# Removal keys and keys transposed two chunks at a time in the RWKV-7 part of a one-core decoder trunk

## The chip, the cores and the metric

One NeuronCore of a Trainium2 chip runs the whole layer. The metric is the device time of one execution in microseconds (us). A change of less than about 0.2% cannot be told from none here.

## The reference

One layer of a hybrid decoder trunk on 1024 tokens of width 1024: `h += W_out [ HGRN2 | dilated window attention | RWKV-7 ]( W_in rmsnorm(h) )`, then a gated feed-forward with a causal convolution, then a gated per-token embedding, then a final RMSNorm. All in float32. The change is in RWKV-7 alone, four heads of 64:

```
def step(state, inp):
    r_t, w_t, k_t, v_t, kk_t, a_t = inp
    sa = jnp.einsum('bhvk,bhk->bhv', state, -kk_t)
    state = (state * w_t[:, :, None, :] + sa[..., None] * (kk_t * a_t)[:, :, None, :]
             + v_t[..., None] * k_t[:, :, None, :])
    return state, jnp.einsum('bhvk,bhk->bhv', state, r_t)
```

The kernel does not step through tokens. It takes 16 chunks of 64 tokens and builds, per chunk, small matrices from decayed versions of the removal keys (`-kk`, called `ar[..0..]`), of the receptances (`ar[..1..]`), of `kk*a` (called `bhat` or `be`), and of the keys (`khat` or `kh`), so that the state is carried from chunk to chunk by one matrix product each.

## The kernel before, in words

Features lie on partitions, tokens on the free axis. A pair of heads fills the 128 partitions (64 rows each), so the four heads are two passes, `p` = 0 and 1. Each pass has a preparation (`rwkv_prep`, `rwkv_inverse`: projections, decays, scores and the inverse of a triangular matrix, a long chain on VectorE with two trips through DRAM) and a main part (`rwkv_main`), which calls `rwkv_group` for four groups of four chunks.

A group first needs its operands with tokens on partitions. Before, `block_diag` (L609) copies each operand into a [128, 4, 2, 64] tile whose off-diagonal blocks are zero, head 0 in one half of the columns and head 1 in the other: `abd` from the removal keys by ScalarE (ACT), `bbd` from `bhat` and `kbd` from `khat` by GpSimd (POOL). TensorE then transposes each of the four chunks of each of the three tiles (L754) into a PSUM tile `pt`, and ACT copies each `pt` in one instruction (L755) into `xr` (its columns 0 to 127), `rb` (columns 128 to 255) and `kt`. The values `v` are already done in the other way: two transposes of 128 plain columns (two chunks) each (L758), and four ACT copies of quarters of 64 partitions x 2 chunks x 64 columns (L762), which put each head and chunk in its place in `vt`.

After these come, in this order on TensorE: `py` = AB x T (L785, copied to `Y` by ACT, L786), `sc` = the key scores (L790, which uses `kbd` as its weights), `pu` = the second half of the inverse (L795, waits for `Y`), `pk` (L800), `px` (L806), `pgm` (L813), `pn` (L818 and L819), and the chain over the four chunks (`pS`, `pyo`, L832 to L837), whose result ACT copies into `y` in quarters, as for `v` (L843). All PSUM tiles of this part come from one pool, `mx`, with four buffers; a new tile waits until ACT or VectorE (DVE) has read the one that held its buffer. POOL spreads the scores into `ABt` and half of `rb` (L770) and fills `addend` (L737 to L744).

The order of instructions on each engine is set by the framework's scheduler when the program is built. It fills TensorE's queue between the group's products with the dense projection products of later column blocks (L127, L129, L131, output `dp`), two halves of 512 columns at a time. The engines run their queues in order, so an early product that waits holds everything behind it.

Of the kernel before, what the change touches and what calls it, by code (L numbers as in the profile page):

```python
# [10 lines left out]
F32 = mybir.dt.float32  # L11
# [7 lines left out]
P = 128  # L19
# [60 lines left out]
class Trunk:  # L80
# [429 lines left out]
    def rwkv_prep(self, p, tp, lt, d, j):  # L510

        tc, nc, par = self.tc, self.nc, self.par
# [46 lines left out]
            nc.gpsimd.tensor_tensor(r2, r1, self.mhalf, ALU.pow)  # L559
            d["kr"] = r2  # L560

        ar = self.slots.tile([P, 16, 2, 64], F32, tag="rk_ar", name=self.nm("ar"), bufs=1)
        be, kh = self.slot("bhat"), self.slot("khat")
        d.update(ar=ar, be=be, kh=kh)

# [18 lines left out]
        mxp = self.mxp  # L584
# [4 lines left out]
        v = self.mix_in(4 + 3 * p, 4 + p, "v", hooks={2 * p: removal_keys})  # L589
# [130 lines left out]
    def rwkv_group(self, p, g, rp, d, y3, S):  # L720

        nc, mxp = self.nc, self.mxp
        cs = slice(4 * g, 4 * g + 4)
        ar, v, gC = d["ar"], d["v"], d["gC"]

        def c3(t):
            return t.rearrange("p (c i) -> p c i", i=64)[:, cs, :]

        def rt(name, shape, bufs=1):
            return rp.tile(shape, F32, tag=name, name=self.nm(name), bufs=bufs)  # L730

        ab = self.block_diag(rp, "abd", ar[:, cs, 0, :], nc.scalar)
        bb = self.block_diag(rp, "bbd", c3(d["be"]), nc.gpsimd)
        kb = self.block_diag(rp, "kbd", c3(d["kh"]), nc.gpsimd)
        if (rp, "add") not in self.bd:
            add = rt("addend", [P, 4, 2, 2, 64])
# [5 lines left out]
        for h in (0, 1):  # L742
            q = slice(64 * h, 64 * h + 64)
            nc.gpsimd.tensor_copy(add[q, :, 0, h, :], ar[q, cs, 1, :])  # L744
        abf, bbf, kbf = (t.rearrange("p c a b -> p c (a b)") for t in (ab, bb, kb))

        Xr = rt("xr", [P, 4, 192])
        RB = rt("rb", [P, 4, 256])
        Kt = rt("kt", [P, 4, P])
        Vt = rt("vt", [P, 4, 64])  # L750
        for src, dst in ((abf, Xr[:, :, 0:128]), (bbf, RB[:, :, 128:256]), (kbf, Kt)):
            pt = mxp.tile([P, 4, P], F32, tag="mx", name=self.nm("pt"))
            for u in range(4):
                nc.tensor.transpose(pt[:, u, :], src[:, u, :], self.ident)  # L754
            nc.scalar.copy(dst, pt)  # L755
        pt = mxp.tile([P, 2, P], F32, tag="mx", name=self.nm("pt"))
        for u in (0, 1):
            nc.tensor.transpose(pt[:, u, :], v[:, 256 * g + P * u:256 * g + P * u + P], self.ident)  # L758
        Vt4 = Vt.rearrange("p (b two) v -> p b two v", two=2)
        for h in (0, 1):  # L760
            for c in (0, 1):
                nc.scalar.copy(Vt4[64 * h:64 * h + 64, :, c, :], pt[64 * c:64 * c + 64, :, 64 * h:64 * h + 64])  # L762

        msk = self.msk.rearrange("p (m h i) -> p m h i", h=2, i=64)
        AB = rt("ABt", [P, 4, P])
# [3 lines left out]
        def spread(dst, src, m, eng):  # L769
            eng.tensor_tensor(dst.rearrange("p u (h i) -> p u h i", i=64),  # L770
                              src.unsqueeze(2).broadcast_to([P, 4, 2, 64]),
                              msk[:, m, :, :].unsqueeze(1).broadcast_to([P, 4, 2, 64]), ALU.mult)
# [13 lines left out]
        nc.scalar.copy(Y, py)  # L786
        spread(RB[:, :, 0:128], d["rb"][:, cs, :], 1, nc.gpsimd)
        ps = mxp.tile([P, 4, 2, 64], F32, tag="mx", name=self.nm("sc"))
# [21 lines left out]
        for hh in (0, 1):  # L810
            pg = mxp.tile([P, 2, 256], F32, tag="mx", name=self.nm("pgm"))
            for u in (0, 1):
                nc.tensor.matmul(pg[:, u, :], X[:, 2 * hh + u, 0:128], RB[:, 2 * hh + u, :], start=True, stop=True)  # L813
            nc.vector.tensor_tensor(GM[:, 2 * hh:2 * hh + 2, :], pg, addf[:, 2 * hh:2 * hh + 2, :], ALU.add)
        N = rt("N", [P, 4, 64])
        pn = mxp.tile([P, 4, 64], F32, tag="mx", name=self.nm("pn"))
        for u in range(4):
            nc.tensor.matmul(pn[:, u, :], RB[:, u, 128:256], X[:, u, 128:192], start=True, stop=False)  # L818
            nc.tensor.matmul(pn[:, u, :], Kt[:, u, :], Vt[:, u, :], start=False, stop=True)  # L819
# [3 lines left out]
        for u in range(4):  # L823
            c = 4 * g + u
# [4 lines left out]
            elif c < 15:  # L829
# [3 lines left out]
                nc.vector.scalar_tensor_tensor(Sn, pS, gC[:, c:c + 1], N[:, u, :], ALU.mult, ALU.add)  # L833
            nc.tensor.matmul(py[:, u, :], RB[:, u, 0:128], X[:, u, 128:192], start=True, stop=False)
            nc.tensor.matmul(py[:, u, :], RK[:, u, :], Vt[:, u, :], start=False, stop=S is None)
# [819 lines left out]
```

## Time and profile before

| what | us |
|---|---|
| median of 3 runs | 1521.87 (1519.84 to 1521.97) |
| the profiled execution | 1520.86 |
| its span in the profile | 1519.0 |
| main part of the first pass, by its transposes | about 147 to 217 |
| main part of the second pass | about 350 to 419 |

In the pages and rows PE is TensorE's products, PEld its weight loads, DVE VectorE, ACT ScalarE, POOL GpSimd, SP the queue that issues transfers. A row of the timeline gives start, length, engine, line, operation, output<-inputs, shape, and the count of instructions merged into the row; in brackets stand the idle time of the engine before it and what ended it. [...]

### The profile page before, as it was taken

To read this page: it belongs to the slowest core of one execution; us is meant where nothing else is said; L and a number is where in the kernel's file an instruction comes from. 1 tells how busy PE (TensorE), PEld (TensorE's weight loads), DVE (VectorE), ACT (ScalarE), POOL (GpSimd) and SP (SyncE) were. 2 spreads that over 40 slices of the span, in tenths; PEclk is the share of its full clock that TensorE was granted. 3 is DMA by queue.
4 is the path that set the end of the run, shared out by engine and by line. 5 is a ranking of instruction groups with operands and counts; after the bars stand their busy time and mean duration, and the time that the engine had idled before them with its cause. 6 is when DMAs were issued, how large, how long until landed. Compare 5 with 4: busy or idle time off the path is not lost. (4 is left out here: it accounts for less than half of the span.)

```text
span 1519.0 us, 20098 instructions
## 1 busy us (share of the span) xinstructions
PE 1468.0 (97%) x7452; PEld 1213.5 (80%) x7452; DVE 1087.5 (72%) x1574; ACT 634.8 (42%) x1091; POOL 431.6 (28%) x360
## 2 busy tenths in 40 slices
PE   8999999999999899999999999999999999999995
PEld 7888887888877686778778888888888888888774
DVE  7666443674456578745888888888888799767684
ACT  6533322323324545425454444444444444455541
POOL 2234221315222132113124444444444000003330
PEclk9999999999999999999999999999999999999998
DMA  6124002123052121166333333333333873451352
GB/s 216 56 90 125 15 29 84 56 90 84 1 214 64 70 70 56 43 216 200 111 111 104 104 104 104 105 104 105 104 104 109 308 276 99 123 145 52 109 182 75
DMA packets 78865, 167.82 MB, mean 110 GB/s; under 512 B 19952, under 2 KB 20080, under 8 KB 78768
## 3 DMA queue, kind: packets, MB, share of 16 engines
q1 hardware_dynamic: 64992, 145.44, 29.3%
q10 hardware_dynamic: 12688, 17.04, 3.4%
q0 software_dynamic: 1088, 4.06, 0.8%
q8 instruction: 58, 0.95, 0.3%
q14 instruction: 39, 0.32, 0.1%
HBM read 120.12 MB, written 46.40 MB: 110 GB/s over the span
## 5 line engine op out<-in xcount | busy, mean ns | idle before, releaser
L127 PE MATMUL dp<-xh,whi 128*128 128x512 f32 x544 | 185.7, 399 | 1.4 <-ACT xh L367 1.4
L129 PE MATMUL dp<-xl,whi 128*128 128x512 f32 x544 | 182.8, 393 | 0.4 <-DVE xl L368 0.3
L131 PE MATMUL dp<-xh,wlo 128*128 128x512 f32 x544 | 182.0, 393 | 0.5 <-DVE wlo L106 0.5
L106 POOL TENSOR_TENSOR wlo<-wraw,whi 128x512 fp32r<-128x512 f32 x59 | 80.1, 1358 | 270.7 <-ACT whi L104 266.1
L106 POOL TENSOR_TENSOR wlo<-raw,whi 128x512 fp32r<-128x512 f32 x84 | 134.8, 1623 | 76.2 <-ACT whi L104 76.2
L104 ACT CAST whi<-wraw 128x512 fp32r<-128x512 f32 x120 | 73.1, 618 | 167.6 <-PE dp L129 120.4
L1210 PE MATMUL bg<-t,whi 128*128 128x512 f32 x352 | 133.2, 389 | 0.0
L127 PEld LDWEIGHTS dp<-xh,whi 128*128 128x128 f32 x544 | 100.8, 188 | 24.3 <-issue 3.3
L131 PEld LDWEIGHTS dp<-xh,wlo 128*128 128x128 f32 x544 | 101.8, 188 | 22.1 <-DVE wlo L106 1.3
L129 PEld LDWEIGHTS dp<-xl,whi 128*128 128x128 f32 x544 | 101.6, 188 | 22.2 <-DVE xl L368 1.2
L106 POOL TENSOR_TENSOR wlo<-s,whi 128x512 fp32r<-128x512 f32 x44 | 64.2, 1459 | 172.2 <-ACT whi L104 172.2
L1501 PE MATMUL bg<-t,whi 128*128 128x512 f32 x308 | 95.2, 390 | 0.0
L1501 PE MATMUL bv<-t,whi 128*128 128x512 f32 x308 | 94.9, 389 | 0.0
L104 ACT CAST whi<-raw 128x512 fp32r<-128x512 f32 x88 | 52.7, 620 | 94.9 <-issue 48.5
L104 ACT CAST whi<-s 128x512 fp32r<-128x512 f32 x66 | 38.9, 620 | 122.0 <-PE bg L1210 113.3
L106 DVE TENSOR_TENSOR wlo<-wraw,whi 128x512 fp32r<-128x512 f32 x61 | 50.7, 831 | 43.5 <-ACT whi L104 40.1
L1210 PEld LDWEIGHTS bg<-t,whi 128*128 128x128 f32 x352 | 66.1, 188 | 13.8
L168 POOL TENSOR_TENSOR rst<-rst,mhalf 128x4 f32<-128x4 f32 x8 | 9.8, 1226 | 230.6 <-DVE rst L166 230.6
L1501 PEld LDWEIGHTS bv<-t,whi 128*128 128x128 f32 x308 | 57.8, 188 | 12.0
L1501 PEld LDWEIGHTS bg<-t,whi 128*128 128x128 f32 x308 | 57.8, 188 | 11.8
L1210 PE MATMUL bg<-t,wlo 128*128 128x512 f32 x176 | 67.2, 389 | 0.0
L1497 ACT CAST t<-t 128x512 fp32r<-128x512 f32 x77 | 47.8, 622 | 44.4 <-PE bv L1501 30.3
(406 smaller groups left out, 3702.4 us busy)
## 6 DMA issues: line engine op xcount, KB each, us to landing
raw<-in_ffn_up_dram SPq DMA_DIRECT2D x44, 512.0 KB, 3.7
wraw<-in_w_in_dram SPq DMA_DIRECT2D x29, 512.0 KB, 3.7
z<-zst SPq DMA_DIRECT2D x18, 512.0 KB, 3.1
gb<-ct SPq DMA_DIRECT2D x33, 256.0 KB, 2.0
t<-gb SPq DMA_DIRECT2D x33, 256.0 KB, 2.8
t<-gt SPq DMA_DIRECT2D x33, 256.0 KB, 2.7
zl<-z SPq DMA_DIRECT2D x16, 512.0 KB, 3.5
wraw<-in_ple_gate_dram SPq DMA_DIRECT2D x16, 512.0 KB, 3.7
```

The source lines that it names most:

```text
L104: nc.scalar.copy(hi, src)
L106: eng.tensor_tensor(lo, src, hi.bitcast(F32), ALU.subtract)
L127: nc.tensor.matmul(ps[hf], wh, xh[hf], start=first, stop=False)
L129: nc.tensor.matmul(ps[hf], wh, xl[hf], start=False, stop=False)
L131: nc.tensor.matmul(ps[hf], wl, xh[hf], start=False, stop=last)
L168: nc.gpsimd.tensor_tensor(r2, r, self.mhalf[:, :4], ALU.pow)
L1210: nc.tensor.matmul(ps, w[part == 2][:, s], X[k][part == 1], start=start and k == part == 0, stop=k == 3 and part == 2, skip_group_check=no ...
L1497: nc.scalar.copy(xh, x)
L1501: nc.tensor.matmul(ps[m], wt[part == 2][:, m * P:(m + 1) * P], (xh, xl)[part == 1], start=k == part == 0, stop=k == NK - 1 and part == 2)
```

## The change

The three block-diagonal tiles that were only transposed go: `abd` and `bbd` with their copies altogether; `kbd` stays, since the key scores use it as weights, but is no longer transposed. The removal keys, `bhat`, `khat` and `v` all go through a new inner function `turned`: two transposes of 128 plain columns each into a [128, 2, 128] tile, then four ACT copies of quarters. The zero blocks of `xr`, `rb` and `kt` are cleared once per pass by POOL, when the tiles are made in the first group (`cleared`), and the tiles are kept for all four groups. So that two chunks of removal keys are contiguous, `ar` is stored as [128, 2, 16, 64] and viewed in the old order.

```diff
-        ar = self.slots.tile([P, 16, 2, 64], F32, tag="rk_ar", name=self.nm("ar"), bufs=1)
+        ar = self.slots.tile([P, 2, 16, 64], F32, tag="rk_ar", name=self.nm("ar"), bufs=1).rearrange("p a c i -> p c a i")
...
-        ab = self.block_diag(rp, "abd", ar[:, cs, 0, :], nc.scalar)
-        bb = self.block_diag(rp, "bbd", c3(d["be"]), nc.gpsimd)
         kb = self.block_diag(rp, "kbd", c3(d["kh"]), nc.gpsimd)
...
+        kbf = kb.rearrange("p c a b -> p c (a b)")
+        def cleared(name, n, lo, hi):
+            if (rp, name) not in self.bd:
+                t = self.bd[(rp, name)] = rt(name, [P, 4, n])
+                nc.gpsimd.memset(t[:, :, lo:hi], 0.0)
+            return self.bd[(rp, name)]
+        Xr = cleared("xr", 192, 0, 128)
+        RB = cleared("rb", 256, 128, 256)
+        Kt = cleared("kt", P, 0, P)
         Vt = rt("vt", [P, 4, 64])
-        for src, dst in ((abf, Xr[:, :, 0:128]), (bbf, RB[:, :, 128:256]), (kbf, Kt)):
-            pt = mxp.tile([P, 4, P], F32, tag="mx", name=self.nm("pt"))
-            for u in range(4):
-                nc.tensor.transpose(pt[:, u, :], src[:, u, :], self.ident)
-            nc.scalar.copy(dst, pt)
...
+        def turned(src, dst, o, step):
+            pt = mxp.tile([P, 2, P], F32, tag="mx", name=self.nm("pt"))
+            for b in (0, 1):
+                nc.tensor.transpose(pt[:, b, :], src(b), self.ident)
+            d4 = dst.rearrange("p (b two) v -> p b two v", two=2)
+            for h in (0, 1):
+                q = slice(64 * h, 64 * h + 64)
+                for c in (0, 1):
+                    nc.scalar.copy(d4[q, :, c, o + step * h:o + step * h + 64], pt[64 * c:64 * c + 64, :, q])
+        turned(lambda b: ar[:, c2(b), 0, :].rearrange("p c i -> p (c i)"), Xr, 0, 64)
+        turned(lambda b: d["be"][:, t2(b)], RB, 128, 64)
+        turned(lambda b: d["kh"][:, t2(b)], Kt, 0, 64)
+        turned(lambda b: v[:, t2(b)], Vt, 0, 0)
```

The scheduler sets the queues anew. TensorE's queue in the second group (of four) of the first pass, from its first transpose to `pu`, before:

```order
L754 MATMUL pt_1397<-cst,abd_1242 128x128 x4
L754 MATMUL pt_1403<-cst,bbd_1246 128x128 x4
L754 MATMUL pt_1409<-cst,kbd_1250 128x128 x4
L758 MATMUL pt_1415<-cst,v_692 128x128 x2
L785 MATMUL py_1431<-T_1426,ABt_1422 128x128 x4
L790 MATMUL sc_1438<-ar_483,kbd_1250 128x128 x4
L131 MATMUL dp_1816<-xh_91,wlo_1810 128x512
L795 MATMUL pu_1445<-U_1427,Y_1430 128x128 x4
```

and with the change:

```order
L759 MATMUL pt_1388<-cst,ar_483 128x128 x2
L759 MATMUL pt_1395<-cst,bhat_484 128x128 x2
L759 MATMUL pt_1402<-cst,khat_485 128x128 x2
L129 MATMUL dp_1802<-xl_110,whi_1794 128x512
L129 MATMUL dp_1802<-xl_94,whi_1794 128x512
L759 MATMUL pt_1409<-cst,v_692 128x128 x2
L131 MATMUL dp_1802<-xh_109,wlo_1796 128x512
L131 MATMUL dp_1802<-xh_93,wlo_1796 128x512
L794 MATMUL py_1425<-T_1420,ABt_1416 128x128 x4
L799 MATMUL sc_1432<-ar_483,kbd_1242 128x128 x4
L804 MATMUL pu_1439<-U_1421,Y_1424 128x128 x4
```

Six transposes are gone, and four dense products stand among the rest where one stood. ACT's queue for the same group, before:

```order
L755 COPY xr_1393<-pt_1397 128x4x128
L755 COPY rb_1394<-pt_1403 128x4x128
L755 COPY kt_1395<-pt_1409 128x512
L762 COPY vt_1396<-pt_1415 64x2x64 x4
L617 COPY abd_1242<-ar_483 64x4x64
L786 COPY Y_1430<-py_1431 128x512
```

and with the change:

```order
L764 COPY xr_1254<-pt_1388 64x2x64 x4
L764 COPY rb_1256<-pt_1395 64x2x64 x4
L764 COPY kt_1258<-pt_1402 64x2x64 x4
L764 COPY vt_1387<-pt_1409 64x2x64 x4
L795 COPY Y_1424<-py_1425 128x512
```

Three copies became twelve, and the `abd` copies are gone. POOL's queue at the start of the second pass's main part, before:

```order
L612 MEMSET abd_2762 128x512
L612 MEMSET bbd_2766 128x512
L612 MEMSET kbd_2770 128x512
L617 COPY bbd_2766<-bhat_2088 64x4x64 x2
L617 COPY kbd_2770<-khat_2089 64x4x64 x2
L737 MEMSET addend_2774 128x1024
L770 TENSOR_TENSOR ABt_2811<-sc_2351,cst 128x512
L739 COPY addend_2774<-cst 128x128 x4
L744 COPY addend_2774<-ar_2087 64x4x64 x2
```

and with the change:

```order
L612 MEMSET kbd_2748 128x512
L735 MEMSET addend_2752 128x1024
L617 COPY kbd_2748<-khat_2075 64x4x64 x2
L737 COPY addend_2752<-cst 128x128 x4
L742 COPY addend_2752<-ar_2073 64x4x64 x2
L748 MEMSET xr_2760 128x4x128
L748 MEMSET rb_2762 128x4x128
L748 MEMSET kt_2764 128x512
L779 TENSOR_TENSOR ABt_2795<-sc_2337,cst 128x512
```

`ABt`, the operand of `py`, moved from ahead of the two rows that fill `addend` to behind all of the set-up, and `xr`, whose copies on ACT wait for its clearing, is cleared after `addend` is filled. In TensorE's queue the eight transposes of this first group moved ahead by 47 dense products, while `py` stayed where it was, two dense products later.

More of the change, by code (lines that the diff above doesn't have):

```diff
@@ L744, in rwkv_group @@
             nc.gpsimd.tensor_copy(add[q, :, 0, h, :], ar[q, cs, 1, :])
[L745 to L749, printed above, removed]
-        Vt = rt("vt", [P, 4, 64])
-        for src, dst in ((abf, Xr[:, :, 0:128]), (bbf, RB[:, :, 128:256]), (kbf, Kt)):
-            pt = mxp.tile([P, 4, P], F32, tag="mx", name=self.nm("pt"))
-            for u in range(4):
-                nc.tensor.transpose(pt[:, u, :], src[:, u, :], self.ident)
-            nc.scalar.copy(dst, pt)
@@ L756, in rwkv_group @@
[L756 to L762, printed above, removed]
+        kbf = kb.rearrange("p c a b -> p c (a b)")
[4 more added lines that the diff above has]
+            return self.bd[(rp, name)]
@@ L764, in rwkv_group @@
+        c2 = lambda b: slice(4 * g + 2 * b, 4 * g + 2 * b + 2)
+        t2 = lambda b: slice(256 * g + P * b, 256 * g + P * b + P)
+        turned(lambda b: ar[:, c2(b), 0, :].rearrange("p c i -> p (c i)"), Xr, 0, 64)
+        turned(lambda b: d["be"][:, t2(b)], RB, 128, 64)
+        turned(lambda b: d["kh"][:, t2(b)], Kt, 0, 64)
+        turned(lambda b: v[:, t2(b)], Vt, 0, 0)
         msk = self.msk.rearrange("p (m h i) -> p m h i", h=2, i=64)
```

## The prediction

> **What bounds the kernel now.** I read the page first, then the windows by stage, then the timeline of the main parts.
>
> ```profile
> PE 1468.0 (97%) x7452; PEld 1213.5 (80%) x7452; DVE 1087.5 (72%) x1574; ACT 634.8 (42%) x1091; POOL 431.6 (28%) x360
> ```
>
> TensorE is busy for 97% of the span: its queue sets the time. The windows are the main part of the first pass, that of the second, and a stage behind both; after the bounds stands the window's length, then the busy time of PE, PEld, DVE, ACT and POOL.
>
> ```profile
> 146.90:217.00 70.10, 67.91 (x484) 60.90 (x483) 32.99 (x59) 25.73 (x67) 18.87 (x26) 1.00 0.05 16
> 345.00:419.00 74.00, 71.99 (x507) 65.35 (x506) 33.81 (x60) 28.39 (x74) 31.04 (x45) 1.00 0.15 37
> 494.00:608.00 114.00, 103.31 (x724) 83.27 (x724) 82.17 (x149) 60.90 (x118) 26.14 (x21) 0.94 0.19 65
> ```
>
> In the main parts (the first two rows) TensorE's busy time is a little short of the window, so it waits there. In those parts every product removed is time gained, and every wait added is time lost. The second group of the first pass, all of TensorE and ACT from the first transpose to `pu`:
>
> ```profile
> 163.35 0.61 PE L754 MATMUL pt<-cst,abd 128*128 128x128 f32 x4
> 163.80 0.60 PE L754 MATMUL pt<-cst,bbd 128*128 128x128 f32 x4
> 164.05 0.59 ACT L755 COPY xr<-pt 128x512 f32<-128x512 f32 x1 [7.78 <-PE pt L754]
> ...
> 164.69 0.44 PE L758 MATMUL pt<-cst,v 128*128 128x128 f32 x2
> 165.01 0.60 ACT L755 COPY kt<-pt 128x512 f32<-128x512 f32 x1
> 165.18 1.16 PE L785 MATMUL py<-T,ABt 128*128 128x128 f32 x8
> 165.49 1.09 ACT L762 COPY vt<-pt 64x128 f32<-64x128 f32 x4
> 166.18 1.06 PE L790 MATMUL sc<-ar,kbd 128*128 128x128 f32 x8
> 166.99 0.48 PE L131 MATMUL dp<-xh,wlo 128*128 128x512 f32 x1
> 167.02 0.59 ACT L786 COPY Y<-py 128x512 f32<-128x512 f32 x1
> 167.66 1.16 PE L795 MATMUL pu<-U,Y 128*128 128x128 f32 x8 [0.19 <-ACT Y L786]
> ```
>
> Four transposes take 0.45 us from start to start, 0.11 each. ACT starts 0.37 us after the last transpose of a tile starts. Three whole copies take 1.44 us from `xr`'s start to `vt`'s, so one hands over after 0.48 us, though it lasts 0.59; four quarters take 1.09 and the next instruction starts only behind them. `pu` starts 0.05 us after `Y` ends. So ACT's copies, not TensorE, end last ahead of `pu`. The other seven groups, first transpose and `pu`:
>
> ```profile
> 146.93 0.60 PE L754 MATMUL pt<-cst,abd 128*128 128x128 f32 x4
> 151.23 0.94 PE L795 MATMUL pu<-U,Y 128*128 128x128 f32 x6 [0.36 <-ACT Y L786]
> ...
> 179.81 0.61 PE L754 MATMUL pt<-cst,abd 128*128 128x128 f32 x4
> 186.33 0.94 PE L795 MATMUL pu<-U,Y 128*128 128x128 f32 x6 [0.80 <-ACT Y L786]
> ...
> 200.81 0.60 PE L754 MATMUL pt<-cst,abd 128*128 128x128 f32 x4
> 204.69 1.16 PE L795 MATMUL pu<-U,Y 128*128 128x128 f32 x8
> ...
> 350.56 0.60 PE L754 MATMUL pt<-cst,abd 128*128 128x128 f32 x4
> 354.62 1.05 PE L795 MATMUL pu<-U,Y 128*128 128x128 f32 x8
> ...
> 366.15 0.61 PE L754 MATMUL pt<-cst,abd 128*128 128x128 f32 x4
> 370.64 1.16 PE L795 MATMUL pu<-U,Y 128*128 128x128 f32 x8 [0.50 <-ACT Y L786]
> ...
> 383.02 0.61 PE L754 MATMUL pt<-cst,abd 128*128 128x128 f32 x4
> 387.51 1.16 PE L795 MATMUL pu<-U,Y 128*128 128x128 f32 x8 [0.50 <-ACT Y L786]
> ...
> 401.14 0.60 PE L754 MATMUL pt<-cst,abd 128*128 128x128 f32 x4
> 405.06 1.11 PE L795 MATMUL pu<-U,Y 128*128 128x128 f32 x8
> ```
>
> The eight stretches are 4.30, 4.31, 6.52, 3.88, 4.06, 4.49, 4.49 and 3.92 us, together 35.97. By the queue's order 2, 1, 6, 0, 1, 0, 0 and 0 dense products lie inside, which are needed anyway:
>
> ```profile
> 136.04 0.62 PE L127 MATMUL dp<-xh,whi 128*128 128x512 f32 x2
> 136.50 0.62 PE L129 MATMUL dp<-xl,whi 128*128 128x512 f32 x2
> ```
>
> Two take 0.46 us, so one is 0.227, and the ten are 2.27. Without them the stretches cost 33.70 us. That is the sum to set against the change.
>
> **The change part by part.** *Transposes.* 14 per group become 8: six less, 0.65 us, or 5.2 us over eight groups, all of it on the bounding engine. This is inside the stretches below.
>
> *ACT's copies.* Three copies of 0.48 us become three times four quarters of 1.09. The shape is that of `vt` (64 partitions, 128 elements from PSUM), so I take its price. The bounds per tile are 0.48 (a whole copy) and 1.09. The chain from first copy to `Y` grows by 1.83 us per group. The two `abd` copies that go (0.4 us each) help little, since the scheduler had put them behind `vt` or `Y`.
>
> *The regular group, by the new order*, from its first transpose: ACT starts at 0.11 + 0.37 = 0.48; `xr` is done at 1.57, `rb` 2.66, `kt` 3.75, `vt` 4.84, `Y` 5.43, so `pu` starts at 5.48. TensorE has 8 transposes (0.87), `py` and `sc` (0.9 each) and the dense products between, four in the second group: 3.58 us of work. It waits for the rest: the transposes of `v` for the buffer that `xr` frees, `py` for that of `rb`, `sc` for that of `kt`, `pu` for `Y`. Everything behind these on TensorE waits too.
>
> *All eight groups.* First pass: 5.97 (an activation of a projection, some 0.5 by the whole copies, stands between `xr` and `rb`), 5.48, 5.78 (`sc` waits for `vt` at 4.84, then runs 0.9), 5.48. Second pass: its first group below, then 6.35 twice (four `y` quarters of the group before, 1.09, stand ahead of `xr` and start at 0.26), and 5.48.
>
> *First group of the second pass.* The eight transposes moved 47 dense products ahead, but POOL cannot start its set-up earlier than before:
>
> ```profile
> 346.30 0.53 POOL L612 MEMSET abd<- 128x512 f32 x1 [10.06 <-DMA Uz<-Ub]
> ...
> 348.62 0.84 POOL L617 COPY kbd<-khat 64x256 f32<-64x256 f32 x2
> 349.52 0.95 POOL L737 MEMSET addend<- 128x1024 f32 x1
> 350.55 1.28 POOL L770 TENSOR_TENSOR ABt<-sc,cst 128x512 f32<-128x512 f32 x1
> 351.78 2.00 POOL L739 COPY addend<-cst 128x128 f32<-128x128 f32 x4
> 353.73 1.38 POOL L744 COPY addend<-ar 64x256 f32<-64x256 f32 x2
> ...
> 349.05 0.62 ACT L104 CAST whi<-wraw 128x512 fp32r<-128x512 f32 x1
> ```
>
> In the new order: 346.30 + 0.53 (`kbd`) + 1.03 (`addend`) + 0.90 + 1.95 + 1.38 + 0.53 gives `xr` cleared at 352.6; two more clearings and `ABt` end at 354.9, where they ended at 351.8. TensorE comes to `py` at 350.56 + 0.87 + 0.45 = 351.9 and waits 3.0 us for `ABt`. ACT's sixteen quarters run from 352.6 to 357.0, two casts follow (0.62 long, taken as handing over 0.09 earlier, as whole copies do by 0.11: 1.06), then `Y`: `pu` at 358.7. The stretch is 8.14 us. In the first pass the same set-up is covered: it would end about 144, and the transposes come at 146.9.
>
> *Sum.* 5.97 + 5.48 + 5.78 + 5.48 + 8.14 + 6.35 + 6.35 + 5.48 = 49.03 us, with 6, 4, 7, 4, 3, 5, 5 and 4 = 38 dense products inside (8.63): 40.40 against 33.70, **6.7 us lost**, the transposes' gain already counted.
>
> *The clock.* The wait of 3.0 us, followed by one of 1.8, has a price of its own. After a wait of 2.03 us the granted clock was 0.50:
>
> ```profile
> 551.36 2.04 PE L1099 MATMUL swo<-pT,sV 128*64 128x128 f32 x24 [2.03 <-DVE zl L1003]
> ...
> 552.30:555.60 3.30, 3.30 (x26) 2.97 (x23) 2.77 (x5) 2.26 (x5) 0.00 (x0) 0.50 0.21 79
> ```
>
> 3.3 us at half clock lose up to 1.7 us; as part of it would fall into the second wait I take 0.9, between 0 and 1.7. [...]
>
> *At nothing:* POOL's `bbd` copies (idle behind them but for the first group); the layout of `ar` (as many elements for DVE, and `sc` reads two runs of 64 instead of one of 128); up to 0.8 us either way for both together, in the range.
>
> The profiled execution took 1520.86 us, 1.0 below the median shown; 1520.86 + 6.7 + 0.9 = **1528.5 us**.
>
> **The rivals.** *1. The quarters overlap (faster).* Whole copies hand over 0.11 us before their end. If the quarters (0.26) did too, a tile would take 0.61, regular groups would be bound by TensorE's own 2.67 us, or 2.8 where `y` comes first, and the late group by POOL at 5.5: 24.6 against 33.70, less 9.1 us: 1512. For it: the whole copies. Against it: four quarters of this very shape took 1.09. It decides below about 0.9 us per tile, where gain and loss are even. [...]
>
> *2. Given back later (about the same).* In the window 494 to 608 TensorE is idle for 10.7 of 114 us while DVE has 82 of work. If DVE works ahead while the main part is late, some 5 us come back: 1523. Against it: that stage takes its buffers and inputs from the RWKV part and starts as late as it.
>
> *3. More waits (slower still).* The half clock comes twice at its full 1.7 us, and `pk` in the third group waits for the `y` copies too (1 us): 1533.
>
> **How the numbers follow.** Forecast, 1525 to 1532: 0.59. Rival 1: 0.16. Rival 2: 0.18. Rival 3: 0.07. A change counts from 0.2% (3 us), about what a measurement here can tell. Faster is rival 1, 0.16; same is rival 2, 0.18; slower is the rest, 0.66. The range 1520 to 1533 leaves out rival 1 and half of rival 3.
>
> **What would show it.** Quarters of `xr`, `rb`, `kt` at about 1.09 per four; `pu` some 5.5 us behind the first transpose in regular groups, waiting for `Y`; `py` waiting some 3 us for POOL's `ABt` once; a window of half clock right after it. I am wrong if four quarters hand over in less than 0.9, if `ABt` of the second pass comes before 353, or if the stages from 420 on are shorter by what the main parts lost.

## The result, and the profile after

The changed kernel takes 1525.64 us (median of 16 runs), the one before 1521.09 us (16 runs): a ratio of 1.0031, with a 95% interval from 1.0023 to 1.0038. It is slower, by some 4.6 us; 7.6 were forecast. Its profiled execution took 1521.16 us and is the shortest of its 16, so its own end says little; its stages do.

The first line of the page after, and the same two stretches by windows (the second is 80 us here, since the part ends later):

```profile
PE 1459.8 (96%) x7404; PEld 1203.8 (79%) x7404; DVE 1083.3 (71%) x1574; ACT 641.8 (42%) x1147; POOL 426.0 (28%) x346
...
146.90:217.00 70.10, 63.99 (x436) 55.52 (x433) 32.34 (x58) 30.14 (x98) 16.89 (x20) 1.00 0.11 39
345.00:425.00 80.00, 71.58 (x473) 62.12 (x472) 33.31 (x60) 30.83 (x98) 25.65 (x36) 1.00 0.16 39
```

The 48 transposes are gone (7404 products instead of 7452). In the first stretch TensorE is now, by its busy time, idle for 6.1 of 70.1 us where it was idle for 2.2. Products in a row are timed by the distance of their starts: in this trace pairs of dense ones start every 0.45 us, and the row of a pair lasts 0.62. The second group of the first pass, from the timeline after:

```profile
164.61 0.39 PE L759 MATMUL pt<-cst,ar 128*128 128x128 f32 x2
...
165.09 1.12 ACT L764 COPY xr<-pt 64x128 f32<-64x128 f32 x4 [7.56 <-PE pt L759]
...
166.23 1.11 ACT L764 COPY rb<-pt 64x128 f32<-64x128 f32 x4
166.26 0.44 PE L759 MATMUL pt<-cst,v 128*128 128x128 f32 x2 [0.36 <-ACT xr L764]
...
167.37 1.11 ACT L764 COPY kt<-pt 64x128 f32<-64x128 f32 x4
167.44 1.13 PE L794 MATMUL py<-T,ABt 128*128 128x128 f32 x8 [0.28 <-issue]
...
168.50 1.08 ACT L764 COPY vt<-pt 64x128 f32<-64x128 f32 x4
...
169.60 0.59 ACT L795 COPY Y<-py 128x512 f32<-128x512 f32 x1
...
170.24 1.16 PE L804 MATMUL pu<-U,Y 128*128 128x128 f32 x8 [0.53 <-ACT Y L795]
```

ACT is busy without a gap from 165.09 on: four tiles of four quarters, one tile every 1.14 us, then `Y`, and `pu` 0.05 us behind its end. `pu` comes 5.63 us after the first transpose, where it came after 4.31. The first group of the second pass:

```profile
341.73 0.38 PE L759 MATMUL pt<-cst,ar 128*128 128x128 f32 x2
...
350.57 1.00 POOL L737 COPY addend<-cst 128x128 f32<-128x128 f32 x4
...
351.52 0.85 POOL L742 COPY addend<-ar 64x256 f32<-64x256 f32 x2
352.43 0.53 POOL L748 MEMSET xr<- 128x512 f32 x1
...
352.99 1.11 ACT L764 COPY xr<-pt 64x128 f32<-64x128 f32 x4 [10.84 <-DMA Tc<-Uz]
...
353.96 1.26 POOL L779 TENSOR_TENSOR ABt<-sc,cst 128x512 f32<-128x512 f32 x1
...
354.12 1.11 ACT L764 COPY rb<-pt 64x128 f32<-64x128 f32 x4
...
355.28 1.16 PE L794 MATMUL py<-T,ABt 128*128 128x128 f32 x8 [1.40 <-ACT rb L764]
...
359.30 1.16 PE L804 MATMUL pu<-U,Y 128*128 128x128 f32 x8 [1.74 <-ACT Y L795]
```

`xr`'s transposes stand done for 11 us until its tile is cleared at 352.96 (the bracket of its copy names a transfer, but the copy starts 0.03 us behind the clearing); then `py` waits 1.40 us and `pu` 1.74. `ABt` ends at 355.22 and the copy of `rb`, which frees the buffer that `py` needs, at 355.23: both hang on POOL's set-up, and this trace cannot say which of the two held `py`. How far behind the kernel is after both main parts is read from the first product of the attention stage, `swq` (L1063 before, L1072 after). The first `swq` of its second pair of heads waits for a load (`zl`). Before, then after:

```profile
445.06 0.48 PE L1063 MATMUL swq<-zl,zl 64*128 64x128 f32 x2
...
528.74 0.80 PE L1063 MATMUL swq<-zl,zl 64*128 64x128 f32 x4 [4.01 <-DMA zl<-z]
```

```profile
452.00 0.48 PE L1072 MATMUL swq<-zl,zl 64*128 64x128 f32 x2
...
533.38 0.49 PE L1072 MATMUL swq<-zl,zl 64*128 64x128 f32 x4 [1.85 <-DMA zl<-z]
```

The main parts cost 6.94 us, and 2.3 of them are gone by the second pair of rows. So two questions: are the 7 us those of the forecast, and why do some come back?

### The profile page after: what moved, and what is told of

It reads as the page before. It is cut to its first block, busy times and chain, and to the rows that moved or that the text cites. A ratio compares the mean times of both kernels' runs of the same rounds, so it can differ in the third digit from the quotient of the medians.

```text
span 1519.4 us, 20078 instructions
## 1 busy us (share of the span) xinstructions
PE 1459.8 (96%) x7404; PEld 1203.8 (79%) x7404; DVE 1083.3 (71%) x1574; ACT 641.8 (42%) x1147; POOL 426.0 (28%) x346
```

## The experiments

All ratios are to runs of the kernel before on the same chip. The last column is the time of the first `swq` in the profile, less its mean in three traces of the kernel before (444.71): the price of the main parts alone (for "quarters, 14 transposes" with a half clock inside, see below).

| kernel | median us | ratio, 95% interval | first `swq`, us |
|---|---|---|---|
| the change, again | 1524.91 | 1.0032 (1.0019 to 1.0044) | +7.0 |
| quarters shared by ACT and DVE | 1516.66 | 0.9979 (0.9971 to 0.9987) | -0.6 |
| quarters, 14 transposes | 1526.87 | 1.0042 (1.0030 to 1.0054) | +10.6 |
| the change, POOL's set-up first | 1521.44 | 1.0006 (0.9997 to 1.0014) | +4.3 |
| shared quarters, set-up first | 1513.26 | 0.9955 (0.9941 to 0.9969) | -3.9 |
| tiles alternating, set-up first | 1513.29 | 0.9955 (0.9941 to 0.9969) | -4.8 |
| whole copies, 8 transposes, set-up first | 1511.00 | 0.9944 (0.9928 to 0.9959) | -5.6 |
| the kernel before, tiles alternating | 1518.51 | 0.9986 (0.9976 to 0.9996) | -2.2 |
| quarters, 14 transposes, set-up first | 1523.87 | 1.0023 (1.0014 to 1.0032) | +7.0 |

**The change again.**

> The changed kernel itself, for a second trace. Theory (the main parts lose some 7 us to ScalarE's quarters and GpSimd's set-up, and a later stage that waits for VectorE gives some back): first transpose to pu again 5.4 to 6.5 us in every regular group, the first dwv-attention product (swq) again 7 us later than before, and about 3 us of it gone by 535 us; median 4 to 5 us above before. Rival (the 3 us came back only because this profile had fewer stretches of half clock): swq 7 us late, and still 6 to 7 us late after 660 us in an execution with as many stretches of half clock as before.

The stretches from first transpose to `pu` are the same to 0.02 us, and `swq` is late by 7.0 us; the median is 3.9 us above the kernel before. What is given back is taken up below.

**Half of the quarters on VectorE.**

```diff
-                    nc.scalar.copy(d4[q, :, c, ...], pt[64 * c:64 * c + 64, :, q])
+                    (nc.scalar.copy if h == 0 else nc.vector.tensor_copy)(d4[q, :, c, ...], pt[64 * c:64 * c + 64, :, q])
```

> Half of the quarters (those of head 1, of all four operands) go to VectorE, so that ScalarE issues two per tile and not four. Nothing is left out. Theory (ScalarE's chain sets pu): a tile takes 0.55 us on ScalarE, a regular group from first transpose to pu 3.3 to 4.2 us instead of 5.5 to 6.5, so 1.5 to 2 us less in each of seven groups and 10 to 13 us less than the change: 1512 to 1516, under before. Rival (VectorE, which is busy with the spreading of T, U, AKt, RKt and the casts, holds its quarters up): xr, rb and kt are ended by VectorE, the stretch stays at 5 us or more and the time within 3 us of the change. In both, the first group of the second pass still waits for GpSimd.

1516.66 us: 8 to 9 us less than the change and 4.3 under the kernel before, just above the theory's 1512 to 1516 and far from the rival. The second group of the first pass:

```profile
164.23 0.55 ACT L764 COPY xr<-pt 64x128 f32<-64x128 f32 x2 [7.56 <-PE pt L759]
...
164.81 0.55 ACT L764 COPY rb<-pt 64x128 f32<-64x128 f32 x2
164.81 0.59 DVE L764 COPY xr<-pt 64x128 f32<-64x128 f32 x2 [0.80 <-ACT xr L764]
...
168.05 1.16 PE L804 MATMUL pu<-U,Y 128*128 128x128 f32 x8
```

ACT now hands over a tile every 0.58 us, and `pu` waits for nothing: 4.30 us after the first transpose at 163.75, with five dense products inside where there was one. Seen in the second and third rows, VectorE starts its half of a tile only when ACT has ended the other half: one tile is no faster, but the next one follows sooner. That, and a wait of 2.2 us ahead of `py` in the first group of the second pass that stays, is what I put the missing part of the expected 10 us down to; it was not tried apart. The first `swq` comes 7.7 us sooner than in the change (mean of its three traces), which makes up for all that the change loses there: the chain of quarters on ACT is the main cause of the loss.

**The quarters without the change.** The kernel before, with `xr`, `rb` and `kt` cleared once and filled in quarters of 64 x 128 out of its own 14 transposes:

```diff
-            nc.scalar.copy(dst, pt)
+            for h in (0, 1):
+                q = slice(64 * h, 64 * h + 64)
+                for b in (0, 2):
+                    nc.scalar.copy(dst[q, b:b + 2, q], pt[q, b:b + 2, q])
```

> The kernel before with its block-diagonal tiles and its 14 transposes per group, but ScalarE moves xr, rb and kt in four quarters of 64 x 128 elements each, into tiles that GpSimd cleared once per pass, as the change does. Nothing is left out. Theory (the copies are what costs, the transposes give 5.2 us back): the main parts lose 7 us as the change does and another 5.2 us that the transposes gave, less what GpSimd's longer set-up changes: 1530 to 1535 median. Rival (the loss is from the plain layout, the new order of the queue or the missing tiles, not from the copies): within 3 us of before, 1518 to 1524.

1526.87 us is 5.9 us above the kernel before, which refutes the rival, but short of the theory's 1530. The first `swq` comes 3.5 us later than in the change; the medians lie only 2.0 us apart, with intervals that overlap. Its quarters are also not those of the change. Each copies between the same 64 partitions, first two in one half, then two in the other, and four of them take 0.87 us. Four of the change, each of which reads the other half than the one before it, take 1.07 to 1.12, and so do the quarters of `vt` here, which alternate too. ACT in the second group of the first pass:

```profile
165.11 0.87 ACT L764 COPY xr<-pt 64x128 f32<-64x128 f32 x4 [7.77 <-PE pt L760]
166.00 0.87 ACT L764 COPY rb<-pt 64x128 f32<-64x128 f32 x4
166.90 0.87 ACT L764 COPY kt<-pt 64x128 f32<-64x128 f32 x4
167.79 1.07 ACT L771 COPY vt<-pt 64x128 f32<-64x128 f32 x4
```

A tile is handed over after 0.89 us here and after 1.14 in the change: 0.75 us less for three tiles, or up to 6 us over the eight groups, which is more than the transposes cost. So this run does show that such copies lose time without the change, but not how much the transposes are worth under the change's own quarters. In its second pass the wait that I had forecast for the change does occur, with a half clock behind it (the timeline, and a window behind the wait; the figure after the five busy times is the granted clock):

```profile
358.45 2.08 PE L794 MATMUL py<-T,ABt 128*128 128x128 f32 x8 [3.59 <-POOL ABt L779]
...
358.50:361.50 3.00, 3.00 (x14) 3.00 (x15) 0.85 (x1) 1.87 (x7) 3.00 (x3) 0.50 0.00 0
```

**POOL's set-up in another order.** In the source, `cleared` moves ahead of `kbd`, and the spreading of `ABt` ahead of `addend`; the queues of TensorE and ACT stay.

> The changed kernel with GpSimd's set-up in another order: xr, rb and kt cleared first, then kbd cleared and ABt, and addend last. TensorE's and ScalarE's queues are the same as in the change, instruction for instruction. Theory: in the first group of the second pass ScalarE's quarters start 4 us earlier and ABt ends 3.7 us earlier, so the two waits of 1.4 and 1.7 us ahead of py and pu go, and the time is 3.0 to 3.5 us less than the change: 1522 median. Rival (ScalarE's quarters hold this group anyway, or the stage behind gives this loss back): within 1 us of the change, 1525.

3.5 us under the change, as the theory says. `ABt` is ready 3.8 us sooner, and `pu`, which still waits 0.40 us for `Y`, comes 2.9 us sooner:

```profile
350.10 1.28 POOL L748 TENSOR_TENSOR ABt<-sc,cst 128x512 f32<-128x512 f32 x1
350.12 1.11 ACT L776 COPY xr<-pt 64x128 f32<-64x128 f32 x4 [8.09 <-POOL kbd L612]
...
356.44 0.82 PE L804 MATMUL pu<-U,Y 128*128 128x128 f32 x5 [0.40 <-ACT Y L795]
```

**Both together.**

> Half of the quarters on VectorE, and GpSimd's set-up in the order that clears xr, rb and kt first, forms ABt next and fills addend last. Theory (the two losses are separate, and add up): the wait of 2.3 us for ABt in the first group of the second pass goes, and the time is 2 to 3.5 us under that with the split alone: 1513 to 1514.5. Rival (the stage behind gives it back, or VectorE holds that group): within 1 us of the split alone, 1516 to 1517.5.

1513.26 us: 3.4 less than the split alone, and the wait ahead of `py` is gone. In the split alone it was not a wait for `ABt`, though the expectation has it so: `ABt` had ended 2.1 us before `py` started, and `T`, which VectorE spreads behind its quarters, only 0.3 us before. POOL's order reaches it by way of the quarters. The two losses add up (at the first `swq` 7.7 and 2.8 us apart, 11.0 together), and without them the change gains 0.45%.

**Whole tiles alternating** (`rb` and `vt` wholly on VectorE, `xr` and `kt` wholly on ACT, set-up first):

> As the kernel with the split and the set-up first, but whole tiles alternate: xr and kt by ScalarE, rb and vt by VectorE, all four quarters of a tile on one engine. In the split VectorE's two quarters of a tile started only when ScalarE's two of the same tile had ended. Theory (the two engines write one tile one after the other, so work on different tiles side by side is better): rb starts within 0.3 us of xr's start, the wait of the transposes of v (0.45 to 0.5 us per group) shrinks, and the time is 1 to 2.5 us under the split with the set-up first: 1511.5 to 1513. Rival (the four tiles need 2.2 to 2.4 us either way, and VectorE's other work decides): within 1 us of it.

```profile
164.44 1.11 ACT L776 COPY xr<-pt 64x128 f32<-64x128 f32 x4 [7.56 <-PE pt L771]
164.60 1.20 DVE L776 COPY rb<-pt 64x128 f32<-64x128 f32 x4 [0.38 <-PE pt L771]
165.57 1.11 ACT L776 COPY kt<-pt 64x128 f32<-64x128 f32 x4
165.60 0.44 PE L771 MATMUL pt<-cst,v 128*128 128x128 f32 x2 [0.35 <-ACT xr L776]
```

`rb` does start beside `xr`, but the transposes of `v` wait as before for the buffer of `xr`, which takes 1.11 us either way; 1513.29 us is the rival's answer.

**The transposes alone.** One whole copy per tile out of the two blocks read twice; the rearrangement is left out, so the part's numbers are not those that are needed.

```diff
+            if step:
+                nc.scalar.copy(d4[:, :, :, o:o + 128], pt.unsqueeze(2).broadcast_to([P, 2, 2, P]))
+                return
```

> The changed kernel with the set-up first, but xr, rb and kt are filled by one ScalarE copy of 128 x 512 elements each, as before, out of the two transposed blocks read twice: the rearrangement is left out, so that what xr, rb and kt hold is not what the part needs. Eight transposes per group as in the change, ScalarE's chain as in the kernel before. Theory (TensorE's own work is the bound once the copies are short): the six transposes less are worth 0.65 us per group, the first swq comes some 5 us earlier than before, and the time is 1515 to 1517. Rival (the stretch up to pu is set by ScalarE's chain here too, so that transposes less only wait): the gain is 0.2 us per group for the two transposes ahead of the first copy, 1.5 to 2 us in all: 1519 to 1520.

`swq` comes 5.6 us sooner than before, so on TensorE the six transposes are worth their own time once the copies are short. The whole time falls by more, 9.6 us. The shorter wait for `zl` (below) is a part of that; the rest was not traced, since the profiled execution (1514.46 us) is the longest of the six.

**The kernel before, alternating.**

> The kernel before, with its block-diagonal tiles and its 14 transposes, but rb and vt are copied by VectorE and xr and kt by ScalarE. Nothing is left out. Theory (ScalarE's chain already sets pu in the kernel before, so a second engine is worth something without the change): 0.3 to 0.6 us per group less, 1516 to 1518.5, and what the alternating kernel with the change has over it, some 3 to 5 us, is the transposes. Rival (the whole copies are short enough, and the gain of the alternating kernel is the change's alone): within 1 us of before, 1519.5 to 1521.5.

2.4 us under the kernel before (0.9986): its ACT chain, too, was worth something. The alternating kernel with the change is 0.31% or 4.7 us faster still (0.9986 to 0.9955), 2.7 of them by the first `swq`. In these are the eight transposes instead of fourteen, POOL's early set-up and its missing `bbd` copies, which were not tried apart; the rest is behind, the shorter wait for `zl` included.

**Quarters, 14 transposes, set-up first.**

> The kernel before with 14 transposes and ScalarE's quarters, as in the experiment with the quarters alone, but with GpSimd's set-up in the early order. TensorE's queue is that of the quarters alone. Theory (under ScalarE's quarters TensorE waits anyway, so that the transposes are worth 1 to 3 us in all and not 5.2): the wait of 3.6 us for ABt in the first group of the second pass goes, and with it the half clock behind it: 1522.5 to 1524, 1 to 2.5 us above the changed kernel with the set-up first. Rival (the transposes are worth their own time here too): 1526 to 1527, 5 us above it.

1523.87 us, 2.4 above the changed kernel with the same set-up (2.7 at the first `swq`), as the theory says. But its tiles are handed over after 0.89 us and not 1.14 (above), so that two differences stand against each other: fewer transposes, and slower quarters. What the transposes alone are worth under ACT's quarters stays open.

**Two more traces of each kernel, for what comes back.**

> The kernel before itself, for a second trace. In the first trace the wait for the transfer of zl at 524 us was 4.2 us and the half clock behind it lasted 6.8 us; in the four kernels with the change or a part of it the same wait was 1.8 to 2.1 us and the half clock 3.4 us or none. Theory (chance of one execution): here the wait is about 2 us too, and the kernel's time 2 to 4 us under its median. Rival (the later stage gives back what the main parts lose, whatever the execution): the wait is about 4 us again.

> The kernel before, for a third trace. Theory (its wait for zl is longer whatever the execution): 3 us or more, and 6.8 us of half clock behind it. Rival (chance): about 2 us and 3.4 us.

> The changed kernel, for a third trace. Theory (its wait for zl is shorter whatever the execution): 1.8 to 2.1 us, 3.4 us of half clock or none behind it, and the distance to the kernel before falls from 7 us at the first swq to 4 or 5 us at the end. Rival (chance): a wait of 3 us or more, or a distance that stays at 6 to 7 us.

The kernel before waits 4.01, 2.93 and 3.02 us for `zl` (the first expectation has 4.2 for the 4.01 of the row), and each time 6.8 us of half clock follow; the change waits 1.85, 1.74 and 1.80, followed by none, 3.4 and 3.4 us. So it is not chance. Nor does the stage catch up with what it lost: of the five kernels that reach it sooner than the kernel before, four wait 1.66 to 2.16 us too (the fifth, the kernel before with alternating tiles, 3.29).

How much comes back there is read from the last `swq` ahead of the wait and the first `hpo` product behind it: the delay falls from 6.8 to 3.8, from 8.4 to 6.5 and from 5.0 to 3.3 us in the three pairs of traces, by 1.8 to 3.0. Ahead of the wait the pairs differ because single half clocks fall on one side alone: in the second the change has one at 455 us, in the third the kernel before has one at 448.

The windows behind the wait in the first pair, before and after:

```profile
528.80:535.20 6.40, 6.05 (x26) 5.10 (x27) 1.05 (x6) 1.01 (x5) 0.00 (x0) 0.50 0.07 30
```

```profile
533.40:536.80 3.40, 3.04 (x23) 2.52 (x24) 1.05 (x6) 1.03 (x5) 0.00 (x0) 1.00 0.76 300
```

What the transfers show: the same ones are under way, but in the kernel before a load of code (the queue marked "instruction", one packet) falls among them. The transfers from 519 to 529 us before (queue with packets, MB and share; then the two loads that POOL issues, the first of which `swq` waits for, with KB and median us to landing):

```profile
q8 instruction: 1, 0.02, 0.8%
...
zl<-z POOLq DMA_DIRECT2D x2, 512.0 KB, 7.8
```

and from 526 to 533.5 us after, where no such queue is listed:

```profile
zl<-z POOLq DMA_DIRECT2D x2, 512.0 KB, 5.6
```

In all 14 traces of this study the two go together. In the four with a wait of 2.9 us or more (three of the kernel before, one of it alternating) a packet of code starts 2.0 to 2.7 us ahead of the first packet of `zl` and takes about 1 us (1.3 in the longest wait); in the other ten none starts there, but some 5 us ahead or 5 us behind. The records of landings say more: this load reports in 16 parts. In those four traces the last part comes 1.4 to 2.1 us behind the fifteenth, and `swq` starts 0.14 us or less behind that last one; in the other ten it comes at most 0.5 us behind. So the wait is longer by one part of sixteen, which would fit one packet of code in the way of one DMA engine. The change alters how many instructions there are (20078 instead of 20098 in the traces), which may be why the code loads fall elsewhere. Both are the author's guesses: the trace does not name the engine, and no run moved the packet alone. This is a coincidence in 14 of 14, not a shown cause.

## Why the prediction was right, and where it was off

**The bound and the sign: right.** Removed products did not become time, because ACT's copies end last ahead of `pu`. By the first `swq`, the seven microseconds are made of three parts, each from one step between two kernels: fewer transposes with whole copies and POOL's set-up first -5.6, quarters in place of whole copies +9.9 (from -5.6 to +4.3), and POOL's set-up in the change's order +2.8 (from +4.3 to +7.1, the mean of the three traces of the change).

**The regular groups: right.** "`pu` starts at 5.48" became 5.63, and the others were forecast as 5.97, 5.78, 5.48, 6.35, 6.35 and 5.48 us and came as 6.10, 6.04, 5.44, 6.46, 6.46 and 5.57. A tile in quarters took 1.14 us instead of 1.09. The rival of overlapping quarters is refuted for this order of copies: four of them never took less than 1.07. That the price of `vt` held is in part luck: the forecast took it for the shape, but quarters of that same shape took 0.87 where two in a row stay in one half of the partitions, about the 0.9 at which gain and loss were even. Those of `vt` and of the change alternate alike, and four took 1.07 to 1.12 in both.

**The first group of the second pass: right mechanism, too large.** I had ABt end 8.6 us after POOL's start; it took 6.9 (348.30 to 355.22). The six copies into `addend` took 1.85 us instead of the 3.33 that I took from the row before. The waits of 3.0 and 1.8 us became 1.40 and 1.74, and the group's loss against the kernel before (dense products taken off on both sides), forecast as 3.6 us, was 2.4. That was made up by 0.1 us in each other group and a longer wait of `pk` for the `y` copies (1.03 us in the third group, where it had waited 0.36 for another operand; rival 3 had foreseen it), so that 6.7 forecast and 6.9 to 7.2 measured are close by some luck.

**The term for the clock: did not come.** I had booked 0.9 us for a half clock behind a wait of 3.0. The waits were shorter and the clock stayed whole in all three traces of the change (the window from the start of `py`):

```profile
355.30:362.00 6.70, 4.96 (x36) 4.33 (x37) 4.02 (x6) 4.46 (x13) 4.84 (x5) 1.00 0.12 25
```

Where the wait was 3.59 us, in the quarters alone, it came. The stretches of half clock here last 3.4 or 6.8 us, but for the last of each trace. In seven traces half clock also follows waits for `zl` of 1.7 to 2.2 us, 1.4 to 2.4 us after their end; in the first trace of the change there was none behind its 1.85 us, nor behind the 2.04 us ahead of its `swo`, where the kernel before had half clock behind 2.03. So the length of a wait alone did not tell here whether half clock follows.

**The end: the step that failed** is the sum's silence on what lies behind. It carried the 6.7 us to the end unchanged. The "given back later" rival named the right window (494 to 608) with the wrong mechanism: VectorE did not work ahead; one transfer landed sooner and a half clock was shorter. The 1.8 to 3.0 us that come back there are the better part of the 2.9 us between 1528.5 and 1525.64, and the clock term that did not come is the rest. Why the transfer landed sooner stays open.

## What to carry to other kernels

Before trading products on the bounding engine for more, smaller copies, add up the copies between the first product and the next one that needs them all; if that chain is the longer, the saved products only wait. Put such copies on two engines: here the same change then gained 0.21%. And clear and prepare tiles in the order in which they are first needed: in one group of eight, the wrong order on an engine that is 28% busy cost 2.8 us. With both, the change gained 0.45%. Take the price of a copy from one that goes through the partitions in the same order: here four quarters of one shape took 0.87 or 1.1 us.

## What was not expected of the hardware

- Copies of 64 x 128 elements from PSUM overlapped on ACT in one order of partitions and not in another. In the change each reads the other half than the one before it, and four of 0.26 us took 1.07 to 1.12, one starting every 0.27 to 0.29. In the two runs with 14 transposes and quarters, the two that stay in one half start 0.16 us apart though each lasts 0.26, and four took 0.86 to 0.87. Copies of 128 x 512, 0.59 us long, follow each other in 0.48. Whether the change's quarters would overlap in another order was not tried.
- Some rows of POOL and VectorE took longer where the two ran side by side. Before, VectorE's spreading of `T` started with `ABt` on POOL, ended 0.55 us behind it and took 1.82 us; after, POOL's copies ran while VectorE was idle, and `T` took its usual 0.69 (before, then after), while `ABt` took 1.28 and 1.26:

```profile
350.56 1.82 DVE L778 TENSOR_TENSOR T<-Tc,cst 128x512 f32<-128x512 f32 x1 [6.20 <-DMA Tc<-Tz]
```

```profile
352.62 0.69 DVE L787 TENSOR_TENSOR T<-Tc,cst 128x512 f32<-128x512 f32 x1 [6.29 <-DMA Tc<-Uz]
```

So it was with the 1.5 us of the `addend` copies, which the sum had as fixed: the four from `cst` took 1.00 us beside an idle VectorE, and 2.00 before and 1.95 with the set-up first, beside its spreading. Those rows of one engine were a price only beside the same work on the other; why was not shown.
- Two loads of 512 KB landed in 5.6 or 7.8 us at the same place of the program. In the longer case one of their sixteen parts was late, and a code load stood among the transfers.
